# Where the forget gates are clipped in a half head's preparation, and when a filler tile's high and low weight parts are made

## The chip, the cores and the metric

The kernel runs on one core of one Trainium2 chip. The core's engines are PE (TensorE, matrix products, with PEld for its weight loads), DVE (VectorE), ACT (ScalarE), POOL (GpSimd) and SP (SyncE, which issues most DMAs here). The metric is the device time of one execution in microseconds; a measurement gives the median of several executions.

## The reference

One layer of an encoder trunk on 1024 positions of width 1024, all in fp32. A row-normalised input is projected by one combined matrix; the columns feed a convolution module (A), a bidirectional gated scan (B) and two merge gates. The scan has 8 heads of 128 columns, and its forget gates are clipped before the logarithm is taken:

```python
h = _rmsnorm(x, attn_norm_w[layer])
proj = jnp.einsum("bsd,de->bse", h, w_in)
glu_in, q, v, z_f, z_b, og, g_a, g_b = jnp.split(proj, SPLIT_POINTS, axis=-1)
...
f = lb + (1.0 - lb) * jax.nn.sigmoid(zf)
lf = jnp.log(jnp.clip(f, MIN_FORGET, 1.0))
key_gate = (1.0 - lb) * jax.nn.sigmoid(-zf)
...
o = _bi_hgrn2(q, v, z_f, z_b, lb[0], lb[1])
...
return jax.nn.sigmoid(g_a) * a + jax.nn.sigmoid(g_b) * bmix
```

After the mixers come an output projection, a feed-forward block with a gated convolution, and a final normalisation.

## The kernel before

**Products in three parts.** A product of fp32 values is made of three matrix products in a rounded fp32 form. Each operand is split into a high part (a cast, on ACT) and a low part (source minus high part, on DVE); `split` (line 124) issues the two together, and `mm3` multiplies high by high, high by low and low by high (lines 149, 150 and 151). Weights come by DMA into a page `wr` (two of them) and are split into pages `wp` (four).

**The scan.** A head's 1024 positions are two halves of 512, so there are 16 half heads. `scan_inputs` (line 1204) loads the queries and both directions' gates `z`, and lets ACT compute the key gates `kG` (line 1215) and the forget gates `f` (lines 1216 and 1217). Line 1218 then clips `f` for both directions at once, on DVE. It does so when the inputs are requested, a whole half head before `scan_base` (line 1269) uses them. `scan_base` scales the keys (line 1276) and works through block lengths 1, 2, 4, 8 and 16. At each length it first has ACT copy keys and queries in a woven order into pages `A` (line 1228, `woven`), which PE multiplies into scores (line 1247), and then has DVE multiply keys and queries in place by the gates of neighbouring blocks (`double_keys` and `double_queries`, which all show as line 1194, the helper `tt`). `scan_levels` goes on with block lengths 32 and 64, and `scan_states` then has PE transpose the keys (line 1382). So in every half head the chain is: woven copy on ACT, doubling on DVE, next woven copy, and so on, up to the doubling of length 64, and then PE's transposes.

**The fillers.** PE isn't left to wait for that chain. A stream of dense tiles, `dense`, runs between the scan's steps: the remaining columns of the combined projection (gate columns, `rest_jobs`) and the pointwise product of module A. Each is a `std_job`, whose `prep` loads and splits the weight and whose `run` yields after every few products. `between` (line 1531) gives it 1.77 pieces at each of the scan's steps. `run_jobs` prepares the next tile when one begins its last pieces, and at every piece counts down the list `chores`: `later(n, do)` puts a piece of work on it that is issued n pieces later.

**What sets the order.** PE's order is that of the code. The other engines' order is set by a scheduler from dependencies and the written order; each engine works through its own queue in the order that results. `Base.step` issues a half head's first step behind the previous half's last key doubling. Numbers in names below tell buffers apart: `f_912` is one half head's gates, `kG_853` one half head's keys, `wp_923` one high part.

Of the kernel before, what the change touches and what calls it, by code (L numbers as in the profile page):

```python
# [10 lines left out]
F32 = mybir.dt.float32  # L11
# [4 lines left out]
ALU = mybir.AluOpType  # L16
# [18 lines left out]
MIN_FORGET = 1e-6  # L35
# [3 lines left out]
def view(t, off, dims):  # L39

    return bass.AP(
        tensor=t.tensor,
        offset=t.offset + off,
        ap=[list(t.ap[0])] + [list(d) for d in dims],
    )
# [3 lines left out]
def tile_hybrid_encoder(  # L49
# [24 lines left out]
    V, A, G, T = nc.vector, nc.scalar, nc.gpsimd, nc.tensor  # L74

    S, D = x.shape[1], x.shape[2]
    ND = D // P
    CW = conv_dw_w.shape[2]
    CK = conv_dw_w.shape[1]
    NCW = CW // P  # L80
# [14 lines left out]
    def nm(s):  # L95
        uid[0] += 1
        return f"{s}_{uid[0]}"
# [3 lines left out]
    def bank(tag):  # L101
        return ps.tile([P, H], F32, tag=tag, name=nm(tag), bufs=BANKS[tag])

    def page(pool, tag, bufs, dt=F32):
        return pool.tile([P, H], dt, tag=tag, name=nm(tag), bufs=bufs)
# [4 lines left out]
    def ev():  # L110
        return page(mp, "ev", 3)
# [12 lines left out]
    def split(hi, lo, src, eng, late=False):  # L124
        parts = A.copy(hi, src), eng.tensor_tensor(lo, src, hi.bitcast(F32), op=ALU.subtract)  # L125
        if late:
            for i in parts:
                pin(i)
        return hi, lo

    def w_cols(w, r0, nk, c0, cols=P):
        return w[0, r0 : r0 + nk * P, c0 : c0 + cols].rearrange("(k p) e -> p k e", p=P)

    def raw_w(src, nk):
        t = mp.tile([P, nk, P], F32, tag="wr", name=nm("wr"), bufs=2)
        nc.sync.dma_start(t, src)
        return t

    def w_page(nk, pool=None):
        if pool is None:  # L140
            return mp.tile([P, nk, P], F32R, tag="wp", name=nm("wp"), bufs=4)
        return pool.tile([P, nk, P], F32R, tag="wq", name=nm("wq"), bufs=3)

    def mm3(acc, w, act, k, first, last, again=False):


        whi, wlo = w
        ahi, alo = act
        T.matmul(acc, whi[:, k, :], ahi, start=first, stop=False, skip_group_check=again)  # L149
        T.matmul(acc, whi[:, k, :], alo, start=False, stop=False, skip_group_check=again)  # L150
        T.matmul(acc, wlo[:, k, :], ahi, start=False, stop=last, skip_group_check=again)  # L151
# [7 lines left out]
    def later(n, do):  # L159

        chores.append([n, do])
# [86 lines left out]
            while not self.done:  # L248
                self.fill()

    def std_job(src, nk, acts, evac, halves=(0, 1), step=2):


        def prep():
            raw = raw_w(src, nk)
            return split(w_page(nk), w_page(nk), raw, V)

        def run(w, halves=halves):
            for half in halves:
                acc = bank("mm")  # L260
                for k in range(nk):
                    mm3(acc, w, acts(k, half), k, k == 0, k == nk - 1)
                    if k % step == step - 1 or k == nk - 1:
                        yield
                evac(half, acc)

        return prep, run
# [297 lines left out]
    def in_cols(c0):  # L565
        return w_cols(w_in, 0, ND, c0)
# [474 lines left out]
    def lb_of(d, h):  # L1041
        return lbw[:, 2, d * NH + h : d * NH + h + 1]

    def oml_of(d, h):
        return lbw[:, 3, d * NH + h : d * NH + h + 1]
# [91 lines left out]


    rest = todo[2 * NPAIRS :]
    rest_jobs = [std_job(in_cols(c), ND, h_std, e) for c, e in rest[:-2]]  # L1140
    (c0, e0), (c1, e1) = rest[-2:]
    rest_jobs.append(duo_job(in_cols(c0), in_cols(c1), ND, h_std, e0, e1))
    ca = [[None, None] for _ in range(NCW)]
# [8 lines left out]
    def gated_a(i):  # L1152
        def evac(half, acc):
            t = ev()
            nc.sync.dma_start(t, d_ga[i][half])
            V.tensor_tensor(t, acc, t, op=ALU.mult)
            nc.sync.dma_start(d_a[i][half], t)

        return evac

    def pw_col(i):
        return w_cols(conv_pw_w, 0, NCW, i * P)
# [4 lines left out]
    def pw_first():  # L1167
        prep, run = std_job(pw_col(0), NCW, ca_of, gated_a(0))

        def loads():  # L1170
            later(8, lambda: [ca_loads(half) for half in range(2)])
            return prep()

        return loads, run

    rest_jobs.append(pw_first())
    rest_jobs += [std_job(pw_col(i), NCW, ca_of, gated_a(i)) for i in range(1, ND - 2)]
    rest_jobs.append(
        duo_job(pw_col(ND - 2), pw_col(ND - 1), NCW, ca_of, gated_a(ND - 2), gated_a(ND - 1))
    )  # L1180
# [12 lines left out]
    def tt(o, a, b, op=ALU.mult):  # L1193
        return V.tensor_tensor(o, a, b, op=op)  # L1194
# [9 lines left out]
    def scan_inputs(i):  # L1204


        h, half = divmod(i, 2)
        q = page(hp, "q", 2)
        f = hp.tile([P, 2, H], F32, tag="f", name=nm("f"), bufs=2)
        kG = hp.tile([P, 2, H], F32, tag="kG", name=nm("kG"), bufs=3)  # L1210
        nc.sync.dma_start(q, d_q[h][half])
        for d in range(2):
            z = page(hp, "zi", 3)
            nc.sync.dma_start(z, d_z[d][h][half])
            A.activation(kG[:, d, :], z, AF.Sigmoid, scale=-1.0)
            A.activation(z, z, AF.Sigmoid)
            A.activation(f[:, d, :], z, AF.Identity, scale=oml_of(d, h), bias=lb_of(d, h))
        V.tensor_scalar(f, f, MIN_FORGET, 1.0, op0=ALU.max, op1=ALU.min)
        return q, f, kG, kscale[:, h : h + NH + 1 : NH]

    def pairs(t, h, other=H):

        return view(t, 0, [[other + h, 2], [2 * h, H // (2 * h)], [1, h]])

    def woven(t, h):

        t_h = page(hp, "A", 8)
        A.copy(pairs(t_h, h, 0), pairs(t, h))  # L1228
        return t_h
# [22 lines left out]
    def double_keys(kG, tb, h):  # L1252
        n, nb = H // (2 * h), H // h
        return tt(pairs(kG, h), pairs(kG, h), view(tb, 1, [[nb - 1, 2], [2, n], [0, h]]))

    def double_queries(qF, q, tb, h):
        n, nb = H // (2 * h), H // h
        tt(pairs(qF, h), q, view(tb, nb + 1, [[-(nb + 1), 2], [2, n], [0, h]]))

    def totals(tb, h, to=None):  # L1260
        n, nb = H // (2 * h), H // h
        tn = None
        if to is None:
            tn = hp.tile([P, 2, n], F32, tag=f"tb{h}", name=nm("tb"), bufs=1 if h < 8 else 2)
            to = view(tn, 0, [[n, 2], [1, n]])
        tt(to, view(tb, 0, [[nb, 2], [2, n]]), view(tb, 1, [[nb, 2], [2, n]]))
        return tn

    def scan_base(ins):


        q, f, kG, ks = ins
        qF = hp.tile([P, 2, H], F32, tag="qF", name=nm("qF"), bufs=4)
        D_t = hp.tile([P, 4, 32], F32, tag="D", name=nm("D"), bufs=3)
        for d in range(2):
            V.tensor_scalar(kG[:, d, :], kG[:, d, :], ks[:, d : d + 1], None, op0=ALU.mult)
        k_d, Q1 = page(hp, "A", 8), page(hp, "A", 8)
        tt(k_d, kG[:, 0, :], kG[:, 1, :], ALU.add)
        A1 = woven(kG, 1)
        odd = H // 2  # L1280
        tt(
            pairs(Q1, 1, 0),
            view(q, 0, [[1, 2], [2, odd], [1, 1]]),
            view(f, H, [[1 - H, 2], [2, odd], [1, 1]]),
        )
        tt(
            view(qF, 1, [[H - 1, 2], [2, odd]]),
            view(q, 1, [[-1, 2], [2, odd]]),
            view(f, H + 1, [[-(H + 1), 2], [2, odd]]),
        )  # L1290
        double_keys(kG, f, 1)
        double_queries(qF, pairs(Q1, 1, 0), f, 1)
        tb = totals(f, 1)
        yield
        A2, Q2 = woven(kG, 2), woven(qF, 2)
        double_keys(kG, tb, 2)
        double_queries(qF, pairs(qF, 2), tb, 2)
        tb = totals(tb, 2)
        A4, Q4 = woven(kG, 4), woven(qF, 4)
        yield  # L1300
        b = bank("sc")
        for n, (k_t, q_t) in enumerate(((k_d, q), (A1, Q1), (A2, Q2), (A4, Q4))):
            level(slot(b, n), k_t, row(q_t))
        double_keys(kG, tb, 4)
        double_queries(qF, pairs(qF, 4), tb, 4)
        tb = totals(tb, 4)
        A8, Q8 = woven(kG, 8), woven(qF, 8)
        yield
        A.copy(D_t, near(slot(b, 3)))
        for n, m in enumerate((m_d, m_1, m_2)):  # L1310
            V.copy_predicated(D_t, over(m), near(slot(b, n)))
        double_keys(kG, tb, 8)
        double_queries(qF, pairs(qF, 8), tb, 8)
        tb = totals(tb, 8)
        A16, Q16 = woven(kG, 16), woven(qF, 16)
        yield
        double_keys(kG, tb, 16)
        double_queries(qF, pairs(qF, 16), tb, 16)
        tb = totals(tb, 16)
        yield qF, kG, tb, D_t, A8, Q8, A16, Q16  # L1320
# [200 lines left out]
    for h in range(NH):  # L1521
# [4 lines left out]
        for half in range(2):  # L1526
            i = 2 * h + half
# [548 lines left out]
    n = starts[-1] - per_seven - 12  # L2076
# [50 lines left out]
```

## Time and profile before

| What | us |
|---|---|
| median of 3 runs (1707.11 to 1707.71) | 1707.46 |
| the profiled execution | 1706.98 |
| its span, first to last instruction | 1705.0 |
| PE idle, 0 to 497 us (before the scan and its fillers) | 5.87 |
| PE idle, 862 to 1705 us (behind them) | 8.56 |

The span is the time from the first to the last instruction of the profiled execution. PE is the busiest engine, and the two idle sums are the stretch's length less PE's busy time in it. The scan with its fillers lies between these stretches, from about 497 to 862 us. The granted clock of PE was 0.999 of full speed over the whole span.

### The profile page before, as it was taken

How to read it: one execution, taken by the hardware profiler on the slowest of the kernel's cores; microseconds unless marked ns; L12 is line 12 of the kernel's file. 1: busy time of each engine (PE TensorE's matmuls, PEld its weight loads, DVE VectorE, ACT ScalarE, POOL GpSimd, SP SyncE). 2: the span in 40 equal slices, each digit the busy share in tenths (PEclk: the TensorE clock that was granted, in tenths of full speed). 3: DMA queues.
4: the chain of work that ended last, by engine and by line, in shares of the span. 5: the costliest groups of instructions: out<-in, count | busy, mean ns of one | idle time of the engine just before them, and what ended most of it. 6: DMA issues, size and time to landing. Idle time of an engine off the chain costs nothing.

```text
span 1705.0 us, 30406 instructions
## 1 busy us (share of the span) xinstructions
PE 1688.6 (99%) x11719; PEld 1408.2 (83%) x11719; DVE 1269.3 (74%) x1938; ACT 827.3 (49%) x1562; POOL 245.9 (14%) x287
## 2 busy tenths in 40 slices
PE   9999999999999999999999999999999999999998
PEld 6788888888888888888888888888888888888787
DVE  5889899887678888888565467676777776657865
ACT  7454343335476777776432345444344434442334
POOL 1312222200001111111100003122222222000110
PEclk9999999999999999999999999999999999999999
DMA  7887887866573444436797455686777776773842
GB/s 240 284 213 186 191 196 172 205 187 206 165 236 100 139 129 134 129 116 221 241 294 243 128 167 176 153 171 143 172 164 178 164 183 149 237 260 102 212 98 99
DMA packets 332871, 306.17 MB, mean 180 GB/s; under 512 B 17454, under 2 KB 244918, under 8 KB 332726
## 3 DMA queue, kind: packets, MB, share of 16 engines
q1 hardware_dynamic: 285366, 265.42, 48.8%
q0 software_dynamic: 47360, 38.81, 15.4%
q8 instruction: 92, 1.51, 0.4%
q14 instruction: 53, 0.43, 0.1%
HBM read 201.40 MB, written 84.93 MB: 168 GB/s over the span
## 4 chain that ended last, share of the span: by engine, by line
PE 70%; ACT 1%; DVE 1%; DMA 0%; issue 0%; POOL 0%; POOLq 0%; ACTq 0%; DVEq 0%
PE mm L149 16%; PE mm L151 16%; PE mm L150 16%; PE sc L149 3%; PE sc L150 3%; PE sc L151 3%; PE ob L1433 2%; PE tr L149 2%; PE tr L150 2%; PE tr L151 2%; PE sc L1247 1%; PE sc L1333 1%; PE mm L1392 1%; PE sc L1392 1%; PE ob L1247 1%; PE tr L1382 0%
## 5 line engine op out<-in xcount | busy, mean ns | idle before, releaser
L149 PE MATMUL mm<-hx,wp 128*128 128x512 f32 x1068 | 425.7, 399 | 0.0
L151 PE MATMUL mm<-hx,wp 128*128 128x512 f32 x1068 | 417.0, 390 | 0.5 <-DVE wp L125 0.5
L150 PE MATMUL mm<-hx,wp 128*128 128x512 f32 x1068 | 416.2, 390 | 0.6 <-POOL hx L125 0.6
L125 ACT CAST wp<-wr 128x1024 fp32r<-128x1024 f32 (+2 forms) x146 | 146.9, 1006 | 224.3 <-PE mm L150 165.0
L151 PEld LDWEIGHTS mm<-hx,wp 128*128 128x128 f32 x1068 | 200.5, 188 | 44.6 <-DVE wp L125 1.6
L149 PEld LDWEIGHTS mm<-hx,wp 128*128 128x128 f32 x1068 | 200.6, 188 | 40.6 <-ACT wp L125 0.2
L150 PEld LDWEIGHTS mm<-hx,wp 128*128 128x128 f32 x1068 | 200.8, 188 | 39.9 <-POOL hx L125 1.0
L125 DVE TENSOR_TENSOR wp<-wr,wp 128x1024 fp32r<-128x1024 f32 (+2 forms) x144 | 169.5, 1177 | 39.8 <-ACT wp L125 39.4
L1065 DVE SCALAR_TENSOR_TENSOR acc<-gl,v_b,acc 128x1024 f32<-128x1024 f32 x120 | 153.5, 1280 | 1.7
L441 ACT COPY su<-mm 128x512 f32<-128x512 f32 x82 | 47.8, 583 | 84.4 <-PE mm L151 84.3
L1371 POOL DMA_DIRECT2D S<-D x64 | 36.1, 571 | 281.1 <-ACT jk L1438 125.3
L125 ACT CAST wq<-sw 128x1024 fp32r<-128x1024 f32 x41 | 43.2, 1054 | 61.3 <-PE mm L150 32.9
L1194 DVE TENSOR_TENSOR qF<-qF,tb 128x512 f32<-128x512 f32 x96 | 65.9, 686 | 9.5 <-ACT A L1228 8.9
L149 PE MATMUL tr<-hx,wp 128*128 128x512 f32 x180 | 70.1, 390 | 0.0
L151 PE MATMUL tr<-hx,wp 128*128 128x512 f32 x180 | 70.1, 389 | 0.0
L150 PE MATMUL tr<-hx,wp 128*128 128x512 f32 x180 | 70.0, 389 | 0.0
L1194 DVE TENSOR_TENSOR kG<-kG,tb 128x512 f32<-128x512 f32 x96 | 65.9, 687 | 4.0 <-ACT A L1228 2.2
L1710 DVE SCALAR_TENSOR_TENSOR tm<-gp,v_a,tm 128x512 f32<-128x512 f32 x88 | 66.0, 750 | 3.3 <-ACT tm L1708 1.3
L302 POOL DMA_DIRECT2D sw<-in_ffn_w_up_dram x38 | 49.8, 1502 | 116.0 <-DMA sw<-in_ffn_w_up_dram 72.4
L149 PE MATMUL sc<-hy,wq 128*128 128x512 f32 x164 | 63.9, 390 | 0.0
L151 PE MATMUL mm<-hy,wp 128*128 128x512 f32 x164 | 63.8, 389 | 0.0
L149 PE MATMUL mm<-hy,wp 128*128 128x512 f32 x164 | 63.8, 389 | 0.0
(377 smaller groups left out, 3721.9 us busy)
## 6 DMA issues: line engine op xcount, KB each, us to landing
wr<-in_w_in_dram SPq DMA_DIRECT2D x48, 512.0 KB, 5.6
wr<-in_ffn_w_up_dram SPq DMA_DIRECT2D x22, 512.0 KB, 5.6
sw<-in_w_in_dram SPq DMA_DIRECT2D x38, 256.0 KB, 3.1
d_g<-ft SPq DMA_DIRECT2D x38, 256.0 KB, 2.0
sw<-in_ffn_w_up_dram SPq DMA_DIRECT2D x38, 256.0 KB, 3.2
sw<-in_ffn_w_up_dram POOLq DMA_DIRECT2D x38, 256.0 KB, 6.7
wr<-sw POOLq DMA_DIRECT2D x32, 256.0 KB, 3.2
wr<-wr POOLq DMA_DIRECT2D x32, 256.0 KB, 3.3
```

Source lines behind the costliest of these rows:

```text
L125: parts = A.copy(hi, src), eng.tensor_tensor(lo, src, hi.bitcast(F32), op=ALU.subtract)
L149: T.matmul(acc, whi[:, k, :], ahi, start=first, stop=False, skip_group_check=again)
L150: T.matmul(acc, whi[:, k, :], alo, start=False, stop=False, skip_group_check=again)
L151: T.matmul(acc, wlo[:, k, :], ahi, start=False, stop=last, skip_group_check=again)
L302: G.dma_start(o, a, accum_op=ALU.add)
L441: A.copy(t, acc)
L1065: V.scalar_tensor_tensor(acc, g[:, k : k + S], tap(k), acc, op0=ALU.mult, op1=ALU.add)
L1194: return V.tensor_tensor(o, a, b, op=op)
L1247: T.matmul(b[g, o], A_t[:, at : at + 32], Q_t(at), start=True, stop=True)
L1371: G.dma_start(S_t[g : g + 32, :, g : g + 32], D_t[g : g + 32])
L1392: T.matmul(u[:, sl], kTs[d][:, sl], v[:, c, :], start=True, stop=True)
L1710: V.scalar_tensor_tensor(c, g[:, o + k : o + k + H], vec("fdw", k * NF + j), c, op0=ALU.mult, op1=ALU.add,)
```

## The change

A `std_job` can now be made with `apart`. Its high part isn't cast when the weight's load is issued but two pieces of the filler stream later, and its low part one piece after that. All gate tiles behind the first and the single pointwise tiles behind the first are made so; the paired tiles at the end of both lists aren't. And the clip of the forget gates goes from `scan_inputs` to `scan_base`, behind the first woven copy of the keys and ahead of the first use of `f`.

```diff
--- before.py
+++ after.py
@@ -248,12 +248,24 @@
             while not self.done:
                 self.fill()
 
-    def std_job(src, nk, acts, evac, halves=(0, 1), step=2):
+    def std_job(src, nk, acts, evac, halves=(0, 1), step=2, apart=False):
 
 
         def prep():
             raw = raw_w(src, nk)
-            return split(w_page(nk), w_page(nk), raw, V)
+            if not apart:
+                return split(w_page(nk), w_page(nk), raw, V)
+            hi, lo = w_page(nk), w_page(nk)
+
+            def low():
+                V.tensor_tensor(lo, raw, hi.bitcast(F32), op=ALU.subtract)
+
+            def high():
+                A.copy(hi, raw)
+                later(1, low)
+
+            later(2, high)
+            return hi, lo
 
         def run(w, halves=halves):
             for half in halves:
@@ -1137,7 +1149,7 @@
 
 
     rest = todo[2 * NPAIRS :]
-    rest_jobs = [std_job(in_cols(c), ND, h_std, e) for c, e in rest[:-2]]
+    rest_jobs = [std_job(in_cols(c), ND, h_std, e, apart=n > 0) for n, (c, e) in enumerate(rest[:-2])]
     (c0, e0), (c1, e1) = rest[-2:]
     rest_jobs.append(duo_job(in_cols(c0), in_cols(c1), ND, h_std, e0, e1))
     ca = [[None, None] for _ in range(NCW)]
@@ -1174,7 +1186,7 @@
         return loads, run
 
     rest_jobs.append(pw_first())
-    rest_jobs += [std_job(pw_col(i), NCW, ca_of, gated_a(i)) for i in range(1, ND - 2)]
+    rest_jobs += [std_job(pw_col(i), NCW, ca_of, gated_a(i), apart=True) for i in range(1, ND - 2)]
     rest_jobs.append(
         duo_job(pw_col(ND - 2), pw_col(ND - 1), NCW, ca_of, gated_a(ND - 2), gated_a(ND - 1))
     )
@@ -1215,7 +1227,6 @@
             A.activation(kG[:, d, :], z, AF.Sigmoid, scale=-1.0)
             A.activation(z, z, AF.Sigmoid)
             A.activation(f[:, d, :], z, AF.Identity, scale=oml_of(d, h), bias=lb_of(d, h))
-        V.tensor_scalar(f, f, MIN_FORGET, 1.0, op0=ALU.max, op1=ALU.min)
         return q, f, kG, kscale[:, h : h + NH + 1 : NH]
 
     def pairs(t, h, other=H):
@@ -1277,6 +1288,7 @@
         k_d, Q1 = page(hp, "A", 8), page(hp, "A", 8)
         tt(k_d, kG[:, 0, :], kG[:, 1, :], ALU.add)
         A1 = woven(kG, 1)
+        V.tensor_scalar(f, f, MIN_FORGET, 1.0, op0=ALU.max, op1=ALU.min)
         odd = H // 2
         tt(
             pairs(Q1, 1, 0),
```

Lines of the changed kernel below `std_job` carry numbers that are 12 higher (line 1194 is 1206, line 1228 is 1239, line 1218 is now 1291), and the parts made apart show as lines 264 (high) and 261 (low) instead of 125. PE and POOL keep their rows in their order. What moves on the other engines shows at two places.

The first is in the half head whose keys `kG_804` PE begins to transpose at 580.40 us; meanwhile `f_912` is computed for a later half head, and the keys `kG_853` of the next one go through their first doublings. ACT's rows there before:

```order
L1217 ACTIVATE f_912_5784<-zi_915_5792,lbw_1595 128x512
L1452 ACTIVATE tm_876_5560<-tm_876_5560,ors_874_5547 128x128 x2
L1228 COPY A_926_5887<-kG_853_5411 128x2x128x2
L125 CAST wp_923_5872<-wr_922_5870 128x1024
L831 ACTIVATE ev_921_5867<-mm_901_5727 128x512
L1228 COPY A_927_5889<-qF_905_5768 128x2x128x2
L1228 COPY A_929_5895<-kG_853_5411 128x2x64x4
L1546 COPY v_932_5904<-tr_931_5899 128x512
L1228 COPY A_930_5897<-qF_905_5768 128x2x64x4
L1228 COPY A_937_5995<-kG_853_5411 128x2x32x8
```

and now:

```order
L1229 ACTIVATE f_912_5784<-zi_915_5792,lbw_1595 128x512
L1464 ACTIVATE tm_876_5558<-tm_876_5558,ors_874_5545 128x128 x2
L1239 COPY A_926_5884<-kG_853_5411 128x2x128x2
L1239 COPY A_927_5886<-qF_905_5767 128x2x128x2
L843 ACTIVATE ev_921_5866<-mm_901_5726 128x512
L1239 COPY A_929_5892<-kG_853_5411 128x2x64x4
L1239 COPY A_930_5894<-qF_905_5767 128x2x64x4
L1558 COPY v_932_5901<-tr_931_5896 128x512
L264 CAST wp_923_5871<-wr_922_5869 128x1024
L1239 COPY A_937_5994<-kG_853_5411 128x2x32x8
```

The cast of `wp_923` has moved from behind the first woven copy to behind four of them, an eviction and the copy of `v_932`. DVE's rows at the same place before (`wp_924` is the low part to `wp_923`):

```order
L1194 TENSOR_TENSOR kG_804_5094<-kG_804_5094,tb_902_5736 128x2x8x32
L1218 TENSOR_SCALAR f_912_5784<-f_912_5784 128x1024
L1194 TENSOR_TENSOR qF_840_5389<-qF_840_5389,tb_902_5736 128x2x8x32
L1194 TENSOR_TENSOR kG_853_5411<-kG_853_5411,tb_910_5781 128x2x128x2
L125 TENSOR_TENSOR wp_924_5873<-wr_922_5870,wp_923_5872 128x1024
L1194 TENSOR_TENSOR qF_905_5768<-qF_905_5768,tb_910_5781 128x2x128x2
L1194 TENSOR_TENSOR kG_853_5411<-kG_853_5411,tb_928_5893 128x2x64x4
L1194 TENSOR_TENSOR qF_905_5768<-qF_905_5768,tb_928_5893 128x2x64x4
L1194 TENSOR_TENSOR kG_853_5411<-kG_853_5411,tb_936_5993 128x2x32x8
L1462 SCALAR_TENSOR_TENSOR ev_934_5923<-tr_933_5918,v_a_1180,og_892_5695 128x512
L1194 TENSOR_TENSOR qF_905_5768<-qF_905_5768,tb_936_5993 128x2x32x8
```

and now:

```order
L1206 TENSOR_TENSOR kG_804_5094<-kG_804_5094,tb_902_5735 128x2x8x32
L1206 TENSOR_TENSOR qF_840_5388<-qF_840_5388,tb_902_5735 128x2x8x32
L1206 TENSOR_TENSOR kG_853_5411<-kG_853_5411,tb_910_5781 128x2x128x2
L1206 TENSOR_TENSOR qF_905_5767<-qF_905_5767,tb_910_5781 128x2x128x2
L1206 TENSOR_TENSOR kG_853_5411<-kG_853_5411,tb_928_5890 128x2x64x4
L1206 TENSOR_TENSOR qF_905_5767<-qF_905_5767,tb_928_5890 128x2x64x4
L261 TENSOR_TENSOR wp_924_5872<-wr_922_5869,wp_923_5871 128x1024
L1206 TENSOR_TENSOR kG_853_5411<-kG_853_5411,tb_936_5992 128x2x32x8
L1474 SCALAR_TENSOR_TENSOR ev_934_5922<-tr_933_5917,v_a_1180,og_892_5694 128x512
L1206 TENSOR_TENSOR qF_905_5767<-qF_905_5767,tb_936_5992 128x2x32x8
```

The clip of `f_912` has left its place behind the first row, and the low part has moved down past three doublings and stands right ahead of the third doubling of `kG_853`.

The second is two half heads on, ahead of the transposes at 623.27 us, with the weight parts `wp_1020` and `wp_1021` and the keys `kG_966`. ACT's rows before:

```order
L1410 COPY Sb_962_6118<-mm_1017_6458 128x384
L125 CAST wp_1020_6474<-wr_1019_6472 128x1024
L831 ACTIVATE ev_1018_6469<-mm_1000_6375 128x512
L1216 ACTIVATE zi_1033_6513<-zi_1033_6513 128x512
L1452 ACTIVATE tm_989_6265<-tm_989_6265,ors_987_6252 128x128
L1217 ACTIVATE f_1030_6505<-zi_1033_6513,lbw_1595 128x512
L1452 ACTIVATE tm_989_6265<-tm_989_6265,ors_987_6252 128x128 x3
L1228 COPY A_1039_6598<-kG_966_6122 128x2x128x2
L1228 COPY A_1040_6600<-qF_1023_6489 128x2x128x2
L1228 COPY A_1042_6606<-kG_966_6122 128x2x64x4
L1228 COPY A_1043_6608<-qF_1023_6489 128x2x64x4
L1546 COPY v_1045_6615<-tr_1044_6610 128x512
```

and now:

```order
L1422 COPY Sb_962_6118<-mm_1017_6457 128x384
L1228 ACTIVATE zi_1033_6511<-zi_1033_6511 128x512
L843 ACTIVATE ev_1018_6468<-mm_1000_6374 128x512
L1229 ACTIVATE f_1030_6503<-zi_1033_6511,lbw_1595 128x512
L264 CAST wp_1020_6473<-wr_1019_6471 128x1024
L1464 ACTIVATE tm_989_6264<-tm_989_6264,ors_987_6251 128x128 x4
L1239 COPY A_1039_6597<-kG_966_6122 128x2x128x2
L1239 COPY A_1040_6599<-qF_1023_6486 128x2x128x2
L1239 COPY A_1042_6605<-kG_966_6122 128x2x64x4
L1558 COPY v_1045_6614<-tr_1044_6609 128x512
L1239 COPY A_1043_6607<-qF_1023_6486 128x2x64x4
```

The cast of `wp_1020` has moved behind the sigmoid `zi_1033`, the eviction `ev_1018` and the gates `f_1030`, and the copy of `v_1045` now stands ahead of the woven copy of the queries, `A_1043`. On DVE the low part `wp_1021` stays near its place, one mask further down, and the clip of `f_1030` is gone from behind the masks.

## The prediction

> **What bounds the kernel now.** I read the page first, then the stretch that the change touches, then who waits in it.
>
> ```profile
> PE 1688.6 (99%) x11719; PEld 1408.2 (83%) x11719; DVE 1269.3 (74%) x1938; ACT 827.3 (49%) x1562; POOL 245.9 (14%) x287
> ...
> 497.00:862.00 365.00, 363.02 (x5668) 310.72 (x5667) 301.51 (x655) 258.02 (x598) 51.47 (x80) 1.00 0.49 156
> ...
> PE tr L1382 <- DVE kG L1194: 1.4, 2, 1.1
> PE sc L1247 <- ACT A L1228: 0.6, 1, 0.6
> ```
>
> The first line is busy time by engine: PE works 99% of the span. The second is the stretch from 497 to 862 us, where the scan runs with its filler tiles: PE, PEld, DVE, ACT and POOL busy, then the granted clock, 1.00. PE is busy 363.02 of 365.00 us, so 1.98 us is all that any better order of DVE and ACT can win there. The last two lines name those 2 us: the transposes of the keys wait twice for the last key doubling, 1.4 us in all, and the score matmuls wait once, 0.6 us, for a woven copy that ACT makes. A gain is therefore capped at 2.0 us, 0.12% of the time. A loss isn't capped.
>
> ```profile
> DVE f L1218 <- ACT f L1217: 11.3, 7, 3.6
> DVE wp L125 <- ACT wp L125: 11.2, 8, 3.1
> ...
> L1218 DVE TENSOR_SCALAR f<-f x16: 680/693/697, 488.3 to 784.8; 128x1024 f32<-128x1024 f32 x16
> ```
>
> These are the two waits on DVE that the change aims at: 11.3 us in seven clips that wait for ACT's gates, and 11.2 us in eight low parts that wait for ACT's high part. They are on DVE, and only what reaches PE counts: of these 22.5 us at most 2.0 can.
>
> **The change part by part.** It adds and removes no work: as many clips, casts and subtractions as before, PE's and POOL's rows in the same order. It moves the 16 clips and a few weight parts.
>
> *The clips.* Each leaves the middle of a half head, ahead of the doublings, and comes back behind the two scalings that open its own half. Every half thus loses one clip of 0.69 us and takes in another, earlier, at the place where DVE has just finished the keys that PE transposes. In the halves that open a head this meets slack (rows of the timeline, here and below, ACT's ahead of DVE's ahead of PE's: start, duration, engine, line, operation, what is written<-read, and in brackets the idle time before it with what ended that):
>
> ```profile
> 728.56 0.68 DVE L1194 TENSOR_TENSOR kG<-kG,tb 128x512 f32<-128x512 f32 x1
> ...
> 731.55 0.60 PE L1382 MATMUL tr<-ident,kG 128*128 128x128 f32 x4
> ```
>
> The last doubling ends at 729.24 and PE transposes at 731.55: 2.31 us of cover over a clip of 0.69, so the edit costs nothing there. Without that cover it would cost 0.69 us a half. In the second halves there is hardly any cover, and whether removing the clip helps depends on what stands behind its wait:
>
> ```profile
> 699.69 0.69 DVE L1218 TENSOR_SCALAR f<-f 128x1024 f32<-128x1024 f32 x1 [0.90 <-ACT f L1217]
> ...
> 701.10 0.69 DVE L1194 TENSOR_TENSOR kG<-kG,tb 128x512 f32<-128x512 f32 x1 [0.72 <-ACT A L1228]
> ...
> 708.04 0.55 PE L1382 MATMUL tr<-ident,kG 128*128 128x128 f32 x3 [0.29 <-DVE kG L1194]
> ```
>
> The clip waits 0.90 us for ACT, but the doubling behind it waits a further 0.72 us, again for ACT: it must not overwrite keys before the woven copy has read them. With the clip gone that doubling waits longer and starts at 701.10 all the same, so PE's 0.29 us stays: 0. Only one of PE's three waits has a clip as its direct cause:
>
> ```profile
> 743.15 0.70 DVE L1218 TENSOR_SCALAR f<-f 128x1024 f32<-128x1024 f32 x1 [2.21 <-ACT f L1217]
> ...
> 745.72 0.46 PE L1247 MATMUL sc<-q,A 128*32 128x32 f32 x32
> ...
> 747.36 0.46 PE L1247 MATMUL sc<-A,A 128*32 128x32 f32 x32 [0.59 <-ACT A L1228]
> 748.77 1.23 DVE L125 TENSOR_TENSOR wp<-wr,wp 128x1024 fp32r<-128x1024 f32 x1
> ```
>
> Here DVE is free 2.21 us before the clip, so the chain moves up by about a clip. But in the new order a weight's high part (ACT, 1.06 us in the rows) comes before the woven copy that PE waits for, and its low part (1.23 us, at 748.77 now) before the query doubling that the next copies need. About 0.1 to 0.2 of PE's 0.59 us is won, and as much lost at the transposes that follow. The bounds are -0.6 us (the whole wait goes) and +0.7 us (the low part's 1.23 us less a clip's 0.69, rounded up); I take 0, as both ends have their cause.
>
> *The weight parts, place 1 (half head at 569 to 581).*
>
> ```profile
> 571.59 0.66 ACT L1228 COPY A<-kG 128x512 f32<-128x512 f32 x1
> 572.15 1.06 ACT L125 CAST wp<-wr 128x1024 fp32r<-128x1024 f32 x1
> ...
> 575.71 0.62 ACT L1228 COPY A<-kG 128x512 f32<-128x512 f32 x1
> ...
> 573.24 1.23 DVE L125 TENSOR_TENSOR wp<-wr,wp 128x1024 fp32r<-128x1024 f32 x1 [0.21 <-ACT wp L125]
> 574.39 0.69 DVE L1194 TENSOR_TENSOR qF<-qF,tb 128x512 f32<-128x512 f32 x1
> ...
> 576.42 0.68 DVE L1194 TENSOR_TENSOR kG<-kG,tb 128x512 f32<-128x512 f32 x1
> ...
> 579.66 0.69 DVE L1194 TENSOR_TENSOR kG<-kG,tb 128x512 f32<-128x512 f32 x1
> ...
> 580.40 0.55 PE L1382 MATMUL tr<-ident,kG 128*128 128x128 f32 x3 [1.10 <-DVE kG L1194]
> ```
>
> A clip and its wait go here too, yet the next key doubling needs the copy that ACT starts at 571.59 and ends at 572.25, so it starts near 572.3 as now. The cast, which ACT makes at 572.15 now, comes last of seven operations. They run without a gap from 571.59 to 575.71, so in the other order the cast ends there, or at 575.9 with small waits of its new neighbours. The low part is queued on DVE ahead of the doubling that starts at 576.42 now. It starts at 575.9, takes 1.15 us to the next start (573.24 to 574.39), and that doubling starts at 577.05 to 577.1: 0.65 us late. The operations from there to the last doubling (579.66) stand in the same order and are tied to each other by the woven copies, so it ends about 0.7 us late and PE's wait grows from 1.10 to 1.8 us: **+0.7 us**. The bounds: 0, if the cast runs as early as DVE's new order would let it, and +1.15, the whole low part.
>
> *Place 2 (612 to 623).*
>
> ```profile
> 611.91 1.05 ACT L125 CAST wp<-wr 128x1024 fp32r<-128x1024 f32 x1
> 612.86 0.59 ACT L831 ACTIVATE ev<-mm 128x512 f32<-128x512 f32 x1
> 613.35 0.62 ACT L1216 ACTIVATE zi<-zi 128x512 f32<-128x512 f32 x1
> 613.87 0.39 ACT L1452 ACTIVATE tm<-tm,ors 128x128 f32<-128x128 f32 x1
> 614.17 0.81 ACT L1217 ACTIVATE f<-zi,lbw 128x512 f32<-128x512 f32 x1
> 614.87 0.97 ACT L1452 ACTIVATE tm<-tm,ors 128x128 f32<-128x128 f32 x3
> ...
> 617.54 0.62 ACT L1228 COPY A<-kG 128x512 f32<-128x512 f32 x1 [0.57 <-DVE kG L1194]
> 618.20 0.62 ACT L1228 COPY A<-qF 128x512 f32<-128x512 f32 x1
> 618.72 0.59 ACT L1546 COPY v<-tr 128x512 f32<-128x512 f32 x1
> ...
> 613.00 1.23 DVE L125 TENSOR_TENSOR wp<-wr,wp 128x1024 fp32r<-128x1024 f32 x1 [3.05 <-ACT wp L125]
> 614.14 0.64 DVE L1362 COPY_PREDICATED D<-m,ob 128x128 f32<-128x128 uint8 x2
> ...
> 615.62 0.69 DVE L1194 TENSOR_TENSOR kG<-kG,tb 128x512 f32<-128x512 f32 x1
> ...
> 612.40 0.20 PE L1247 MATMUL ob<-A,A 128*32 128x32 f32 x1
> ...
> 618.08 0.46 PE L1247 MATMUL sc<-q,A 128*32 128x32 f32 x32
> ```
>
> The cast moves behind ev, zi and f. From start to start these take 0.49, 0.52 and 0.70 us, so it runs from 611.91 + 1.71 = 613.62 to 614.67. The low part then starts at 614.7, not 613.00, and takes 1.14 us to the next start; with one mask of 0.32 behind it, the doubling of 615.62 starts at 616.2, 0.58 us late although the clip's 0.69 us are gone. The copy at 617.54 waits for DVE's keys, so it starts at 618.1. Then the copy of v, 0.48 us from start to start, stands ahead of the queries' copy, which runs from about 619.15 to 619.8 in place of 618.82. PE needs it for the last 32 score matmuls. In the rows at 747.36 they were due 747.36 - 0.59 = 746.77, which is 1.05 us behind their group's start (745.72); here that is 618.08 + 1.05 = 619.13. The matmuls started 0.05 us after that copy's end there, so PE waits 619.85 - 619.13: **+0.7 us**. The transposes behind are as late, which covers the doubling that they need. Bounds: 0 (the keys' copy not late, v's fits into slack) and +1.15 (a whole low part).
>
> A page bears on both sums. The Trainium skill, "TensorE: Matmul & The Clock Gate", in the table that opens it, calls the queues of ScalarE and VectorE strict FIFO: what waits at the head holds all behind it. The trace agrees as far as it goes: the masks at 614.14 read what PE had written by 612.60, and yet they stand behind the low part that waited 3.05 us. By that rule the sum is what I have; if DVE could pass a waiting low part, both terms would be 0 and the time 1707.0.
>
> *The rest.* On SP, one weight load falls behind a store:
>
> ```profile
> 807.05 0.68 DVE L1156 TENSOR_TENSOR ev<-mm,ev 128x512 f32<-128x512 f32 x1
> ...
> 825.27 0.60 ACT L125 CAST wp<-wr 128x512 fp32r<-128x512 f32 x1
> ```
>
> The store waits for the first row, done at 807.73, and the loaded weight is cast in the second: 17 us of cover. It would cost what the load is late by, under 5 us, if the cast were due at once; I take 0. The other parts that move do so by a few rows among work with margin.
>
> **Sum.** The profiled execution took 1706.98 us: its span of 1705.0 and 1.98 around it. To this come 0 for the clips, 0 for the place at 747, and 0.7 + 0.7 for the two places: 1706.98 + 1.4 = **1708.4 us**, 0.08% more. That execution stood 0.48 us below the median of the runs shown (1707.46), which is within their spread from 1707.11 to 1707.71.
>
> **The rivals.**
>
> *The waits go and PE's with them.* All three of PE's waits (1.10, 0.29, 0.59) vanish: 1706.98 - 1.98 = 1705.0 us. For it: DVE waits 22.5 us at just these two kinds of place. Against it: behind two of the three stands ACT, as the rows at 701.10 and at 571.59 show. Chance 0.2.
>
> *Nothing that PE sees.* The moved parts meet slack in the new run too, because ACT's and DVE's waits shift against each other by a few tenths: 1707.0 us. For it: PE's order is the same, most parts keep their row, and my two terms are differences of chains worked out by hand. This is also what follows if the change doesn't do what it says, since the scheduler had put most casts behind their load already. Chance 0.22.
>
> *Slower: late low parts hold the doublings.* Each second half has next to no cover at its transposes (0.05 us at 580.40, where the wait had ended). If a late high part leaves the low part at the head of DVE's queue ahead of the keys not in two of them but in six or seven of the eight, at 0.7 us each, the sum is 4.2 to 4.9 us: 1711.2 to 1711.9. It decides for slower from five such halves on, 5 x 0.7 = 3.5 us. Against it: only at these two places does the order put a high part behind copies that the doublings don't need. Chance 0.08.
>
> **How the numbers follow.** Forecast 0.5, the rivals 0.2, 0.22 and 0.08. Own range of the forecast: 1707.3 (half of one term) to 1709.3 (both at 1.15). With the gain at 1705.0, less the 0.3 us by which runs spread, and half the way to the slower rival, the range is 1704.7 to 1710.6. A measurement of this kernel tells about 0.2%, or 3.4 us, from no change: faster would be under 1704.0, slower above 1710.9. The cap of 2.0 us leaves faster 0.04; slower has 0.08; the rest, 0.88, is within.
>
> **What would show it.** In the profile of the changed kernel, the clip's wait for ACT's f should be gone from DVE's list, while the wait of the key doublings for ACT's copies grows; the transposes near 581 should wait about 1.8 us, the score matmuls near 619 about 0.7 us, and the transposes near 709 still 0.3 us. PE's idle time from 497 to 862 should be 3.4 us rather than 1.98. The forecast is wrong if that idle time falls below 1.5 us, since then ACT wasn't what stood behind the clips, or if it passes 5 us, since then low parts hold DVE at more places.

## The result and the profile after

The changed kernel is slower by a little: 1709.61 us median of 22 runs (1708.61 to 1710.21) against 1707.12 us of the kernel before, 22 runs too (1706.49 to 1707.92). The ratio is 1.0014, with a 95% interval from 1.0008 to 1.0020. That is 2.49 us; 1.4 us were forecast.

The first block shows, of the changed kernel, the busy time by engine, the stretch with the scan (length, then PE, PEld, DVE, ACT and POOL busy), and who PE waited for in it. The lines in the code are 12 higher than before, or 11 for the weaving copies and the score matmuls.

```profile
PE 1689.5 (99%) x11719; PEld 1408.4 (82%) x11719; DVE 1268.2 (74%) x1938; ACT 827.1 (48%) x1562; POOL 247.3 (14%) x287
...
497.00:862.00 365.00, 361.13 (x5656) 308.88 (x5655) 298.22 (x653) 256.79 (x596) 53.00 (x80) 1.00 0.48 153
...
PE tr L1394 <- DVE kG L1206: 2.7, 3, 1.5
PE sc L1258 <- ACT A L1239: 1.2, 2, 0.7
```

PE now idles 365.00 - 361.13 = 3.87 us where it idled 1.98, and both kinds of wait are those of before, grown from 1.4 and 0.6 us to 2.7 and 1.2. The granted clock is 1.00 in this stretch in both, so the clock isn't what made the time longer. POOL's busy time has grown too, from 51.47 to 53.00 us, though its work is the same. The next blocks are a line of DVE's list of waits before, and then the list and the clip's own group now.

```profile
DVE kG L1194 <- ACT A L1228: 2.2, 5, 0.7
```

```profile
DVE kG L1206 <- ACT A L1239: 12.5, 9, 3.1
...
DVE qF L1206 <- ACT A L1239: 9.2, 11, 2.1
DVE wp L261 <- ACT wp L264: 8.4, 7, 2.0
...
DVE wp L125 <- ACT wp L125: 2.0, 2, 1.7
...
L1291 DVE TENSOR_SCALAR f<-f x16: 673/682/696, 487.4 to 799.0; 128x1024 f32<-128x1024 f32 x16
...
  ACT f L1229: 1.2, 1
```

The clip did what it was moved for: of 11.3 us of waiting for ACT's gates 1.2 are left. But the key doublings' wait for ACT's woven copies has gone from 2.2 to 12.5 us. What DVE no longer waits ahead of the clip (10.1 us) it waits one row further on (10.3 us). The low parts' wait, 11.2 us before, has hardly changed: 8.4 us in those made apart and 2.0 in the others. Five matmuls show what reached PE, from the timeline:

```profile
580.73 0.55 PE L1394 MATMUL tr<-ident,kG 128*128 128x128 f32 x3 [1.51 <-DVE kG L1206]
...
619.99 0.46 PE L1258 MATMUL sc<-A,A 128*32 128x32 f32 x32 [0.48 <-ACT A L1239]
...
709.82 0.55 PE L1394 MATMUL tr<-ident,kG 128*128 128x128 f32 x3 [1.01 <-DVE kG L1206]
...
749.28 0.46 PE L1258 MATMUL sc<-A,A 128*32 128x32 f32 x32 [0.69 <-ACT A L1239]
...
753.92 0.55 PE L1394 MATMUL tr<-ident,kG 128*128 128x128 f32 x3 [0.18 <-DVE kG L1206]
```

The half heads that end in these places are the ones that grew. From one half's transposes to the next half's, by the starts of their first matmul in the timelines:

| half head that ends at | before, us | after, us | longer by | of it, longer waits |
|---|---|---|---|---|
| 580.73 | 561.13 to 580.40: 19.27 | 561.03 to 580.73: 19.70 | 0.43 | 0.41 |
| 624.28 | 603.91 to 623.27: 19.36 | 604.27 to 624.28: 20.01 | 0.65 | 0.48 |
| 709.82 | 689.57 to 708.04: 18.47 | 690.61 to 709.82: 19.21 | 0.74 | 0.72 |
| 753.92 | 731.55 to 751.66: 20.11 | 733.35 to 753.92: 20.57 | 0.46 | 0.28 |

Together these are 2.28 us, of 2.41 by which the scan grew from the first half head's transposes to the last one's (519.17 to 836.10 before, 519.05 to 838.39 after). The other eleven of these fifteen stretches make up 0.13 us. Where a half head grew by more than its waits, the last section says why.

### The profile page after: what moved, and what is told of

It reads as the page before. It is cut to its first block, busy times and chain, and to the rows that moved or that the text cites. A ratio compares the mean times of both kernels' runs of the same rounds, so it can differ in the third digit from the quotient of the medians.

```text
span 1707.5 us, 30417 instructions
## 1 busy us (share of the span) xinstructions
PE 1689.5 (99%) x11719; PEld 1408.4 (82%) x11719; DVE 1268.2 (74%) x1938; ACT 827.1 (48%) x1562; POOL 247.3 (14%) x287
## 3 DMA queue, kind: packets, MB, share of 16 engines
q8 instruction: 92, 1.51, 0.4%
## 4 chain that ended last, share of the span: by engine, by line
PE 68%; ACT 2%; DVE 2%; issue 1%; POOL 0%; DMA 0%; POOLq 0%; ACTq 0%; DVEq 0%
PE mm L149 16%; PE mm L151 16%; PE mm L150 16%; PE sc L149 3%; PE sc L150 3%; PE sc L151 3%; PE ob L1445 2%; PE tr L149 1%; PE tr L150 1%; PE tr L151 1%; PE sc L1258 1%; PE sc L1345 1%; PE mm L1404 1%; PE sc L1404 1%; PE ob L1258 1%
## 5 line engine op out<-in xcount | busy, mean ns | idle before, releaser
L125 ACT CAST wp<-wr 128x1024 fp32r<-128x1024 f32 (+2 forms) x126 | 128.0, 1016 | 215.3 <-PE mm L150 170.1
L125 DVE TENSOR_TENSOR wp<-wr,wp 128x1024 fp32r<-128x1024 f32 (+2 forms) x124 | 147.7, 1191 | 27.3 <-ACT wp L125 21.1
L1206 DVE TENSOR_TENSOR kG<-kG,tb 128x512 f32<-128x512 f32 x96 | 65.7, 686 | 14.6 <-ACT A L1239 12.5
```

## The experiments

Each kernel below was timed in 11 runs beside the kernel before. One such comparison is sure to about 0.09%, or 1.5 us, so a time alone tells few of them from no change; what they show is read from their profiles, one execution each. The table has PE's waits in the scan of 0.15 us and more with their sum, how much longer than before the scan took in the profile (from the first half head's transposes to the last one's), and the difference of the medians, all in us. The first two of the fifteen stretches, which hold none of the places named here, agree within 0.01 us in all these profiles, so the scan's length tells more than the medians do.

| kernel | near 580 | 619 to 624 | near 709 | near 748 | near 753 | sum | scan longer by | time against before |
|---|---|---|---|---|---|---|---|---|
| before | 1.10 | - | 0.29 | 0.59 | - | 1.98 | | |
| the change | 1.51 | 0.48 | 1.01 | 0.69 | 0.18 | 3.87 | +2.41 | +2.49 |
| e1, clip alone | 1.02 | - | 1.00 | 0.71 | 0.18 | 2.91 | +1.37 | +1.47 |
| e2, parts alone | 1.49 | 0.50 | 0.30 | 0.59 | - | 2.88 | +1.06 | +0.91 |
| e3, clip, one half not | 1.10 | - | 0.28 | 0.71 | 0.17 | 2.26 | +0.75 | +0.51 |
| e4, clip, scalings held | 1.02 | - | - | 0.71 | - | 1.73 | +0.49 | +0.57 |
| e8, parts, two tiles not | 1.07 | - | 0.29 | 0.58 | - | 1.94 | -0.05 | -0.16 |
| e12, all but four | 0.99 | - | - | 0.91 | - | 1.90 | +0.69 | -0.04 |
| e5, clip, early copy | 1.22 | - | 1.25 | - | 1.02 | 3.49 | +1.96 | +2.02 |
| e6, before, early copy | 1.21 | - | 0.59 | - | 0.15 | 1.95 | +0.41 | +0.39 |
| e7, change, early copy | 1.76 | 0.34 | 1.25 | - | 1.02 | 4.37 | +2.88 | +2.92 |
| e9, clip, hold | 0.91 | - | 0.99 | - | 0.88 | 2.78 | +0.97 | +0.96 |
| e10, before, hold | 1.08 | 0.29 | 0.93 | - | 0.77 | 3.07 | +1.59 | +1.50 |
| e11, change, hold | 0.90 | 0.48 | 0.99 | - | 0.91 | 3.28 | +1.62 | +1.99 |

**Each half of the change alone.** e1 is the changed kernel without `apart`:

```diff
-    rest_jobs = [std_job(in_cols(c), ND, h_std, e, apart=n > 0) for n, (c, e) in enumerate(rest[:-2])]
+    rest_jobs = [std_job(in_cols(c), ND, h_std, e, apart=False) for n, (c, e) in enumerate(rest[:-2])]
...
-    rest_jobs += [std_job(pw_col(i), NCW, ca_of, gated_a(i), apart=True) for i in range(1, ND - 2)]
+    rest_jobs += [std_job(pw_col(i), NCW, ca_of, gated_a(i), apart=False) for i in range(1, ND - 2)]
```

> The clip move alone, with high and low parts made together as before. Theory (each part of the change costs where it changes ACT's order): the transposes near 709 wait 1.0 us, the score matmuls near 748 wait 0.7 us and the transposes near 753 wait 0.2 us as in the changed kernel, while the wait near 581 is 1.1 us as before and none is at 619: PE waits 3.0 us in the scan against 2.0 before, and the time is 1.0 to 1.3 us above before. Rival (the late low parts cost everything): the time is that of before, within 0.4 us. Rival (the clip was a gain that the parts gave away): 1 us or more below before.

e2 has `apart`, and the clip in `scan_inputs` as before.

> High and low parts made apart, the clip where it was before. Theory: the transposes near 581 wait 1.5 to 1.8 us and the score matmuls near 619 wait 0.5 to 0.7 us; 0.3 us near 708 and 0.6 us near 747 as before; PE waits 2.9 to 3.4 us in the scan, and the time is 0.9 to 1.4 us above before. Rival (the clip move costs everything): no wait near 619, 1.1 us near 580, the time of before.

Both came out as the first theory had it, place by place; e1's time is a little above its range. The clip move owns the waits near 709 and 753, the parts own those near 580 and 619, and neither adds a wait at the other's. The scan's lengths add up, 1.37 + 1.06 = 2.43 us against 2.41 for both. The medians do as well, 1.47 + 0.91 = 2.38 us against 2.49, but each ratio's interval reaches 1 (e1: 1.0008, from 0.9999 to 1.0017; e2: 1.0005, from 0.9996 to 1.0013), so the split rests on the profiles. The rivals fell: neither half was a gain that the other gave away.

**The parts: which tiles.** e8 is e2 with the two tiles left together whose casts change their row:

```diff
-apart=n > 0
+apart=n not in (0, 7, 9)
```

> Parts made apart for all tiles but the two whose casts move at 572 and 612 us, the clip where it was before. Theory: all of the cost of the parts sits in these two tiles: the waits are those of before (1.1 us near 580, none near 619, 0.3 near 708, 0.6 near 747) and so is the time, within 0.4 us. Rival (making parts apart costs something in each tile): 0.5 us or more above before.

The waits are those of before, and so is the scan's length (0.05 us less). So 18 of 20 tiles made apart cost nothing, and all of e2's cost sits in two.

**The clip: why the place near 709.** On ACT, a copy of the backward states (`Sb`, 128x384) has moved from ahead of the scalings of a head's outputs to behind two of them; the scalings wait for two small operations on POOL. e3 keeps one half head's clip in its old place, and with it this copy:

```diff
+        clipped = i in (10,)
+        if clipped:
+            V.tensor_scalar(f, f, MIN_FORGET, 1.0, op0=ALU.max, op1=ALU.min)
+        return q, f, kG, kscale[:, h : h + NH + 1 : NH], clipped
...
+        if not clipped:
+            V.tensor_scalar(f, f, MIN_FORGET, 1.0, op0=ALU.max, op1=ALU.min)
```

> The clip move alone, but not for the half head whose clip the change puts at 690 us: that one stays in its old place, and with it the copy of the backward states stays ahead of the scalings on ACT. Theory: the wait near 709 is back to 0.3 us, the rest as with the clip move alone; the time is 0.7 us below the clip move alone. Rival (the clip that leaves the chain near 699 is to blame, not the one that comes in at 690): the wait near 709 stays 1.0 us.

e4 moves all clips but holds those scalings behind the copy:

```diff
+                behind = tc.issue_after(last_back[0].ins) if h == 3 else ExitStack()
+                with behind:
+                    done = A.activation(
+                        ons[half][:, sl], ons[half][:, sl], AF.Copy, scale=rs[:, half, c : c + 1]
+                    )
```

> The clip move alone, all clips moved, but ACT's scalings of one head's outputs are held behind the copy of the backward states, near 695 us, as they stood before. Theory (of 0.73 us that ACT is late there, 0.36 come from that copy and 0.37 from the small operations on POOL that the scalings wait for): the wait near 709 falls from 1.0 to 0.6 or 0.7 us if both count, to 0.3 us if only the order does, and stays 1.0 us if only the clip's place on DVE and POOL's lateness do.

In e3 the wait is back at 0.28 us, so the clip that comes in at 690 us is the cause, and not the one that left the chain near 699. In e4 it falls to 0.12 us. That is more than I expected, since the hold let the copy and one of ACT's sigmoids both run while ACT waits for POOL, an order better than that of before. The rows of ACT, DVE and POOL there, before (the woven copy last of ACT's):

```profile
694.35 0.47 ACT L1410 COPY Sb<-mm 128x384 f32<-128x384 f32 x1
695.85 1.28 ACT L1452 ACTIVATE tm<-tm,ors 128x128 f32<-128x128 f32 x4 [1.04 <-POOL ors L576]
...
700.44 0.63 ACT L1228 COPY A<-kG 128x512 f32<-128x512 f32 x1
...
693.82 0.34 DVE L1400 SCALAR_TENSOR_TENSOR Sf<-Sf,Tt,sc 128x128 f32<-128x128 f32 x1
...
693.83 0.20 POOL L575 TENSOR_SCALAR ors<-oss 128x8 f32<-128x8 f32 x1 [5.74 <-ACT jk L1438]
694.11 1.71 POOL L576 TENSOR_TENSOR ors<-ors,mhalf 128x8 f32<-128x8 f32 x1
```

and in the changed kernel, with the woven copy and the doubling that follow:

```profile
697.26 0.69 ACT L1464 ACTIVATE tm<-tm,ors 128x128 f32<-128x128 f32 x2 [1.80 <-POOL ors L588]
697.86 0.46 ACT L1422 COPY Sb<-mm 128x384 f32<-128x384 f32 x1
...
702.21 0.64 ACT L1239 COPY A<-kG 128x512 f32<-128x512 f32 x1
...
694.81 0.43 DVE L1206 TENSOR_TENSOR tb<-tb 128x256 f32<-128x256 f32 x1
...
702.89 0.69 DVE L1206 TENSOR_TENSOR kG<-kG,tb 128x512 f32<-128x512 f32 x1 [3.06 <-ACT A L1239]
...
694.85 0.45 POOL L587 TENSOR_SCALAR ors<-oss 128x8 f32<-128x8 f32 x1 [5.73 <-ACT jk L1450]
695.38 1.84 POOL L588 TENSOR_TENSOR ors<-ors,mhalf 128x8 f32<-128x8 f32 x1
```

Against the transposes that open this half (689.57 before, 690.61 after) the scalings start 6.28 and 6.65 us in: 0.37 us late. POOL gives these: its first operation takes 0.45 instead of 0.20 us, and the second, with its start, loses 0.12 more. Then the copy of `Sb` takes 0.36 us (697.86 to 698.22) of a queue that is full from there on, where before it ran while ACT had nothing to do. The sum, 0.73 us, matches what PE's wait grew by (0.29 to 1.01, or 0.72). This division is worked out from the rows; no run takes away one of the two parts and leaves the other as it was. In e4 POOL's operations are as long as in the changed kernel (0.44 and 1.84 us), so with a better order on ACT their delay hardly reaches PE here.

**POOL alone.** e12 undoes the moves at three of the four places and holds the scalings as e4 does; 15 of 16 clips are moved and 18 of 20 tiles made apart:

```diff
-apart=n > 0
+apart=n not in (0, 7, 9)
...
+        clipped = i in (13,)
```

> The change with three of its moves undone and one held: the tiles whose casts move at 572 and 612 us get both parts together, the clip whose move brings a cast ahead of a woven copy near 746 us stays in its old place, and ACT's scalings near 695 us are held behind the copy of the backward states. 15 of 16 clips are moved and 18 of 20 tiles are made apart. Theory (all of the cost sits at these four places): the waits are 1.0 us near 580, none near 619, 0.3 us or less near 708 and 0.6 us near 747; the time is that of before or up to 0.5 us below. Rival (the other moves cost too, each too little to show as a wait of its own): 0.5 us or more above before.

The time is that of before (ratio 1.0001, from 0.9992 to 1.0010), and it doesn't beat it. But the median can't tell a few tenths, and by the profile the scan took 0.69 us longer, so the theory that all of the cost sits at the four places isn't borne out for this kernel. The half heads that end near 751, 794 and 623 are 0.35, 0.25 and 0.19 us longer, those near 580 and 708 are 0.08 and 0.15 shorter. The one near 623 is 0.18 us longer in e1, e3 and e4 too: there the moved clips do cost something, which doesn't show in the changed kernel, where place 2 makes this half head late anyway. The one near 794 isn't longer in the changed kernel (it ends near 797 there). The wait near 748 is 0.91 us, not 0.6, though ACT's and DVE's rows from the scalings to that matmul stand as before. POOL's row before and in e12, and e12's DVE rows beside it:

```profile
735.54 0.59 POOL L575 TENSOR_SCALAR ors<-oss 128x8 f32<-128x8 f32 x1 [4.11 <-ACT jk L1438]
```

```profile
735.38 0.93 POOL L587 TENSOR_SCALAR ors<-oss 128x8 f32<-128x8 f32 x1 [4.12 <-ACT jk L1454]
...
735.37 0.68 DVE L1206 TENSOR_TENSOR qF<-A,f 128x512 f32<-128x512 f32 x1
735.97 0.54 DVE L1206 TENSOR_TENSOR tb<-tb 128x128 f32<-128x128 f32 x2
```

The operation is 0.34 us longer and PE's wait 0.32: here POOL's slowness reaches PE almost whole. DVE's operations beside it are others than before, since the clip that came in shifted them. That these operations are what slows POOL is argued from the rows: no run changes them alone.

**Can the waits be taken away?** Two attempts to get the doublings' copies out of ACT's queue earlier, each with the clip moved, with the kernel before and with the whole change. In e5, e6 and e7 the keys' copy for block length 2 is issued a step earlier:

```diff
         tb = totals(f, 1)
+        A2 = woven(kG, 2)
         yield
-        A2, Q2 = woven(kG, 2), woven(qF, 2)
+        Q2 = woven(qF, 2)
```

> The clip move alone, and with it the woven copy of the keys for block length 2 is issued a step earlier, so that ACT makes it while it waits for POOL instead of behind the gates and scalings. Theory (ACT's order ahead of that copy, not the clip, holds the second halves): the waits near 580 (1.0 us) and near 709 (1.0 us) fall below 0.2 us each, the one near 748 (0.7 us) to 0.3 us or less; the time is 2 to 2.7 us below the clip move alone, 0.5 to 1.5 us below before. Rival (DVE itself is full there): the waits stay within 0.3 us of the clip move alone.

> The kernel before with the same earlier woven copy. Theory: the clip, which waits for ACT's gates ahead of the doublings on DVE, now is what holds them: the waits near 580 and 747 stay above 0.5 us, and the time is 0 to 0.8 us below before, so that the clip's move is worth 0.5 us or more once ACT's copy is out of the way. Rival (the clip's place never matters): the time of the earlier copy with the clip move, within 0.3 us.

> The whole change with the same earlier woven copy. Theory: the late low part still stands ahead of a doubling near 576 and the late cast near 614, but the doublings start earlier, so the waits near 581 and 619 are 0.5 us or less each; the time is 0 to 1 us above that of the earlier copy with the clip move alone and below before. Rival (the low parts hold the chain whatever ACT does): 0.9 us above the earlier copy with the clip move alone.

None of the three theories held. In e5 the score matmuls' wait near 748 went, but the transposes wait longer (1.22, 1.25 and 1.02 us). The keys' copy came early, and the queries' copy stayed behind the gates, the scalings and the weight's cast. In e6 the wait near 747 nearly went (0.06 us left), but those near 580 and 709 grew, and the scan is 0.41 us longer than before; it is 1.96 us longer in e5, so with the early copy the clip is better off in its old place. In e7 the transposes near 581 wait 1.76 us where 0.5 or less was expected. In e9, e10 and e11 the scalings themselves go behind both copies:

```diff
+                if half == 1 and n == 0 and step_of is not None:
+                    step_of.step(1)
+                    with tc.issue_after(last_woven[0].ins):
+                        pending.fill(1)
+                    return
                 pending.fill(1)
```

> The clip move alone, and ACT's scalings of the head's outputs that run ahead of the second halves' first doublings are held behind the woven copies of keys and queries for block length 2. Theory (in the second halves it is ACT's queue that holds the chain of copies and doublings, all of it and not the keys' copy alone): the waits near 580 and 709 fall below 0.4 us each and no new one over 0.3 us comes up; the time is 1.5 to 2.7 us below the clip move alone and 0.5 to 1.5 us below before. Rival (the weight's cast and low part hold the chain there): the waits near 580 and 709 stay above 0.8 us.

> The kernel before with the same hold. Theory: the chain gains too, but the clip, which waits for ACT's gates, still stands in it: PE waits 0.3 to 1.3 us in the scan, the time is 0.3 to 1.5 us below before and above the hold with the clip move. Rival (the clip is no part of it): the time of the hold with the clip move, within 0.2 us.

> The whole change with the same hold. Theory: the cast of place 1 is now back ahead of the queries' copy for length 4, so place 1 costs nothing; place 2 (near 619) still waits 0.3 to 0.5 us; the time is within 0.6 us of the hold with the clip move alone and at or below before. Rival: 0.9 us above it, as the parts made apart cost without the hold.

These fell too: the waits near 580 and 709 stay at 0.91 and 0.99 us in e9, which is what its rival said, and a wait of 0.88 us comes up near 753. The weight's low part isn't the cause that the rival named, though, as the rows below show. In e10 PE waits 3.07 us, and the scan is 1.59 us longer than before against 0.97 in e9: with the hold, the clip's new place is the better one by 0.6 us. In e11 place 2 still waits (0.48 us), as expected, but the time is 1.99 us above before, not at or below it. What e11 kept is that place 1 costs nothing more than in e9 (0.90 against 0.91 us) once the cast is back ahead of the queries' copy. Why the wait near 580 stays shows in e9's rows:

```profile
573.99 1.27 ACT L1464 ACTIVATE tm<-tm,ors 128x128 f32<-128x128 f32 x4
575.17 0.57 ACT L1563 COPY v<-tr 128x512 f32<-128x512 f32 x1
575.63 0.62 ACT L1239 COPY A<-kG 128x512 f32<-128x512 f32 x1
...
572.81 0.68 DVE L1206 TENSOR_TENSOR kG<-kG,tb 128x512 f32<-128x512 f32 x1
...
576.29 0.69 DVE L1206 TENSOR_TENSOR kG<-kG,tb 128x512 f32<-128x512 f32 x1 [1.06 <-ACT A L1239]
```

The keys' doubling for length 4 starts at 572.81 us, where it started at 574.99 before. But the one for length 8, at 576.42 before, starts at 576.29: it waits 1.06 us for a copy that the held scalings now precede. The busy time of PE, PEld, DVE, ACT and POOL in the stretch from 569 to 576 us, before and then in e9:

```profile
569.00:576.00 7.00, 7.00 (x108) 5.71 (x109) 5.25 (x9) 7.00 (x15) 0.00 (x0) 1.00 0.28 87
```

```profile
569.00:576.00 7.00, 7.00 (x101) 5.71 (x101) 5.34 (x9) 7.00 (x15) 0.00 (x0) 1.00 0.23 85
```

ACT is busy all of these 7 us in both. It works 48 or 49% of the whole span, yet in this stretch it is as full as PE, and what isn't ahead of one copy is ahead of the next. Taking work out of ACT there was not tried.

## Why the prediction was right, and where it was short

The direction, the order of size and the range hold, but 2.49 us fall outside the forecast's own range, which ended 2.3 us above the profiled execution. Of the 2.41 us by which the scan grew, 1.08 lie at the two places that the sum had priced and 1.20 at two places that it had put at 0. So the mechanism that was forecast, late weight parts, is right and makes under half of the loss; that the total is still within a factor of two is in part luck. Of the prediction's steps:

- **The cap on the gain** held: no kernel here is faster than before by more than 0.16 us. As a figure it is somewhat low, since it counts idle time alone (see the last section).
- **The clips' wait is replaced by the doublings' wait for ACT** held, as the list of DVE's waits shows.
- **Place 1** was right in mechanism and too large: 0.7 us forecast, 0.43 measured. The late low part started at 575.61, not 575.9, and the doubling behind it at 576.75, not 577.05. I had added 0.2 us for waits of the cast's new neighbours that didn't come.
- **Place 2** was right in mechanism: 0.7 us forecast as a wait. The wait is 0.48 us, the half head 0.65 us longer.
- **"With the clip gone that doubling waits longer and starts at 701.10 all the same, so PE's 0.29 us stays: 0"** failed. This step took ACT's rows ahead of the woven copy as fixed. Against the half's opening the copy came 0.73 us later: 0.36 by a copy that the clip's move had put behind the scalings, a row of ACT's order that I had not walked, and 0.37 by POOL. PE's wait there is 1.01 us, not 0.3, and the half head is 0.74 us longer. This is the largest single miss, and it falls on the edit that was priced at nothing.
- **The place near 747, costed at 0** (bounds -0.6 and +0.7), came out at 0.46 us. The half's first doubling behind the woven copy starts 13.06 us into the half, where it started at 13.41 (746.41 - 733.35 and 744.96 - 731.55), so about half of a clip's length was won there: ACT's woven copy, done by then before, now holds it. With the cast ahead of the queries' copy, as forecast, the score matmuls' wait grew from 0.59 to 0.69 us instead of shrinking, and 0.18 came at the transposes. POOL's operation is longer here too; in e12 it makes 0.32 us of wait alone.
- **The other edits, costed at 0**, held in the changed kernel: outside the four half heads of the table the scan is 0.13 us longer.

POOL's part has a rule. The Trainium skill, "SBUF — State Buffer", section "Who interferes with whom", says that a DVE instruction with two inputs in SBUF (the memory in which the kernel's pages lie) contends with a GpSimd instruction that reads SBUF, and it calls the pair of ports that they share an exclusive lock. The prediction left it out, since no operation of POOL stood on a path that I followed. The trace agrees in kind: the same 128x8 operation takes 0.20 us beside a 128x128 operation on DVE, one of whose inputs (`sc`) PE has written, and 0.45, 0.59 or 0.93 us beside wider ones with two inputs.

## What to carry to other kernels

A wait on an engine which isn't the bottleneck is worth little more than the bottleneck's own idle time behind it: 22.5 us of DVE's waits hung on 2 us of PE's. Before moving work within such an engine's queue, look at which engine ends the next row's wait, and at that engine's load in that stretch rather than over the span. When an edit only moves things, walk the whole order of the other engines in each place with no cover, also the rows that the edit doesn't name: 0.73 of the 2.41 us lost here came, by the rows, from a copy and from two tiny operations that were in none of its lines.

## What the hardware showed that I had not expected

- A 128x8 operation on POOL took 0.20 us alone (at 854.20 us before, with no operation of DVE beside it) and up to 0.93 us beside DVE's operations with two inputs. In the changed kernel it ended 0.06 us behind DVE's 128x256 operation (695.30 and 695.24). In e12 it passed the end of a first such operation (736.05 us) and ended at 736.31 us, 0.06 us behind the end of the next one.
- A new wait costs PE more than the idle time that the profile shows. Near 619 the wait is 0.48 us, and from the group's start (618.08 before, 618.45 after) to the next group (619.36 before, 620.38 after) it takes 1.28 and 1.93 us: 0.65 us more. These matmuls overlap: by the records each lasts about 0.20 us, and the next starts some 0.01 us after it. At the break the next start came 0.68 us later, a whole record and the idle time behind it. It shows even where almost no idle time is left. In e1 the transposes that start at 623.51 have 0.02 us of idle time before them, too little for the table of waits. Yet they waited, for the last key doubling ended 0.06 us before they started, and their half head is 0.18 us longer than before. So a wait that comes up anew costs some 0.17 us beyond its idle time, and one that goes away altogether should win as much. That would raise the cap of 1.98 us for three waits to about 2.5, which is an estimate; no kernel here came near it.

```profile
618.45 0.46 PE L1258 MATMUL sc<-q,A 128*32 128x32 f32 x32
618.73 0.78 PE L1258 MATMUL sc<-A,A 128*32 128x32 f32 x64
...
620.38 0.69 PE L1345 MATMUL sc<-qF,kG 128*64 128x64 f32 x16
```
